# A hybrid decoder block with product-key experts: the scatter of routing weights without accumulation, and 32 instead of 24 tokens by expert rows

## The chip, the cores and the metric

One core of a Trainium2 chip runs the whole program once. The metric is the device time of that core in microseconds (us). A profiled execution gives the trace from which the rows in this text come.

## What is computed

One decoder layer over 512 tokens of width 1024, all in float32: an RMS norm, a joint projection, gated linear attention, sliding-window attention, a gated merge, and then the expert layer, which takes most of the time:

```python
qp = (xt @ w_pq).reshape(t, 8, 2, 128)
scores = einsum('thpd,hpkd->thpk', qp, sub_keys)      # 8 heads, 2 sides, 128 keys
s_top, i_top = top_k(scores, 16)                      # per side
cand = s_top[:, :, 0, :, None] + s_top[:, :, 1, None, :]
best, pos = top_k(cand, 16)                           # 16 experts for each of 8 heads
idx, gate = chosen_experts(pos), softmax(best)        # 128 (expert, weight) pairs per token
h = gelu(einsum('lkd,ld->lk', expert_u[idx], x))
out = einsum('lk,lkd->ld', gate * h, expert_v[idx])   # 16384 experts
```

Two heads of one token can choose the same expert; its weights then add.

## The kernel before

**The experts, two ways.** The 512 tokens are four tiles of 128. Tokens of tile one, and the first `XG` tokens of tile two, go *by expert rows*: for each of a token's 128 experts an indirect DMA fetches that expert's row of U and V side by side (8 KB per token, 1 MB for 128 partitions), VectorE multiplies the U half by the token and sums (`product`, L1339), ScalarE makes the gate, and VectorE adds the gated V half to an accumulator (`addition`, L1356). Tile one takes 128 such *slots* ("v"). The `XG` tokens of tile two are copied `XR = 128 // XG` times over the partitions, so that their 128 experts take only `XS` slots ("y"). With `XG = 24` these are 5 copies, 26 slots, 120 partitions, and 154 slots in all.

The other `TD = 512 - 128 - XG` tokens go *densely*: for each of 128 blocks of 128 experts, `h_step` computes gelu(U·x) of all those tokens (24 matmuls `hp`, line L236, in `proj`), and `v_step` adds V·(weights·h) to eight accumulators (24 matmuls `oa` or `oacc`, L1461). Each number is split in a high and a low part and three products are summed, hence 3 x 8 matmuls of 128x128 weights with `TD` columns. `PHASES` orders the blocks: 88 U blocks, their 88 V blocks, then 20 and 20, then 20 and 20. Each weight block is a 512 KB DMA into `raw`; ScalarE makes its high part `whi`, VectorE its low part `wlo` (L177), some blocks ahead.

**The table of weights.** The dense way needs, for each expert block, a table of 128 experts by tokens that holds the gates. It is built while the first 88 U blocks run. For tokens of tiles two and three VectorE makes two one-hots per token (`onehot`, L1182 and L1185) and TensorE multiplies them (`gmm`, matmuls `gp`, L1198), four tokens at a time, `NGR` groups; ScalarE copies the result to `gbuild` and SyncE writes it to the DRAM tensor `gd`. For tile four the table `g3` lies in DRAM, zeroed early, and GpSimd *scatters* into it: `scatter(h, k)` sends 128 weights, one per token, to the places that `place` computed, with an accumulating indirect DMA (L1153). Within a head a token's experts differ, so its 16 scatters need no order; the first scatter of a head waits for all of the head before (`after`). `HD` says how many scatters are issued after each U block: 16 in 9 blocks. Later `g_load` reads both tables back for four blocks at once (tile `gt`, L1426 and L1427), `w_a` multiplies them with h (L1440, one instruction for each of `PIECES`), and `w_b` makes the low part (L1451).

**The order of the work.** It is written out at build time. `pump` runs steps of the slots between blocks while four counters (`pe`, `dve`, `dma`, `pool`, in estimated us) say that the engines can take them, so an estimate changes the order and nothing else. GpSimd's queue holds scatters and row gathers in one line. In the first stretch at most three row gathers are outstanding (tile `row`, tag `er`); at block 82 all that are outstanding are finished (`while early[0]: step()`), the buffers are freed, and the remaining 126 gathers (tile `rows`, pairs of 2 MB) run beside the V blocks and later U blocks. At block `N0 - GL` = 82 GpSimd issues the first two `g_load`s, which wait for the last head's scatters.

Of the kernel before, what the change touches and what calls it, by code (L numbers as in the profile page):

```python
# [9 lines left out]
F32 = mybir.dt.float32  # L10
# [5 lines left out]
OP = mybir.AluOpType  # L16
# [41 lines left out]
POOLQ = 9.0  # L58
GL = 6

HD = (3, 2, 2, 3, 2, 2, 2, 0, 0)
XG = 24
XR = 128 // XG
XS = -(-128 // XR)
XP_ = XG * XR
# [1 line left out]
TB = 128 - XG  # L67
TD = T - TG

CT, CL = 32, 8  # L70
NGR = (TD - 128) // 4
NCT = (TD - 128 - CL) // CT
GA, GB = NCT * 4 * CT, (1 + 128 // CL) * 4 * CL
# [15 lines left out]
def tile_block(ctx, tc, xT, wst, smalls, wgk2, keysT, uT, vv, uv_rows, out):  # L89
    nc = tc.nc  # L90
# [3 lines left out]
    PS = ctx.enter_context(tc.tile_pool(name="psum", bufs=1, space=PSUM))  # L94
# [102 lines left out]
    for kb in (0, 1, 2, 4, 6):  # L197
        n = 1 if kb < 2 else 2
        nc.sync.dma_start(xt[:, kb:kb + n], xT[:, kb:kb + n])
        if kb < 2:  # L200
            x = slice(kb * 512, kb * 512 + 512)
# [675 lines left out]
    XP = ctx.enter_context(tc.tile_pool(name="xtok", bufs=1, side="left"))  # L877
# [30 lines left out]
    for d in range(9):  # L908
# [12 lines left out]
        if d:  # L921
            p = x1_tail(d - 1)
# [171 lines left out]
    def decode(t):  # L1094
        ij = R.tile([128, 2, 128], F32, name="ij", tag="ij", bufs=2)
        for sd in range(2):
            eq = eq_mult(t, sd)
            yield
            yield from tree(ij[:, sd], eq)
        gf = gate[:, t].rearrange("p h k -> p k h")  # L1100
        if t == 0:
            nc.vector.scalar_tensor_tensor(eidx, ij[:, 0], 128.0, ij[:, 1], OP.mult, OP.add)
            nc.vector.tensor_copy(wgt.rearrange("p (k h) -> p k h", h=8), gf)
            return
        if t == 3:
            nc.vector.tensor_copy(w3.rearrange("p (k h) -> p k h", h=8), gf)
            place(ij)
            return
        eg = R.tile([128, 2, 128], F32, name="eg", tag="eg")
        gk = eg[:, 1]  # L1110
        nc.vector.tensor_copy(gk.rearrange("p (k h) -> p k h", h=8), gf)
        if t == 1:
            nc.vector.scalar_tensor_tensor(eg[:, 0].bitcast(I32), ij[:, 0], 128.0, ij[:, 1], OP.mult, OP.add)

            def copy(r):
                n = min(XS, 128 - r * XS)
                nc.sync.dma_start(misc[r * XG:(r + 1) * XG, 384:384 + 2 * XS].rearrange("p (s k) -> p s k", s=2)[:, :, 0:n],
                                  eg[0:XG, :, r * XS:r * XS + n])

            gout.extend([lambda r=r: copy(r) for r in range(XR)])  # L1120
        yield
        p = PS.tile([128, 3, 128], F32, name="ijp", tag="PT")
        for i, s_ in enumerate((ij[:, 0], ij[:, 1], gk)):
            nc.tensor.transpose(p[:, i], s_, ident)
        ijg = R.tile([128, 3, 128], F32, name="ijg", tag="ijg", bufs=2)
        nc.scalar.copy(ijg, p)
        ijgs[t] = ijg

    addr = XP.tile([128, 128], I32, name="addr")
    scs, heads = [], [[] for _ in range(8)]  # L1130


    def place(ij):
        r4 = R.tile([128, 128], I32, name="r4")
        tk = R.tile([128, 4], I32, name="tk")
        nc.gpsimd.iota(tk[:, 0:1], pattern=[[0, 1]], base=0, channel_multiplier=1)
        nc.vector.tensor_scalar(tk[:, 1:2], tk[:, 0:1], 128 - CL, None, OP.bitwise_and)
        tf = R.tile([128, 4], F32, name="tf")
        nc.vector.tensor_copy(tf[:, 0:2], tk[:, 0:2])
        nc.vector.scalar_tensor_tensor(tf[:, 2:3], tf[:, 1:2], 3.0, tf[:, 0:1], OP.mult, OP.add)  # L1140
        nc.vector.tensor_copy(r4, ij[:, 0])
        nc.vector.tensor_scalar(r4, r4, 3, None, OP.bitwise_and)
        a = ij[:, 1]
        nc.vector.scalar_tensor_tensor(a, ij[:, 0], 32.0, a, OP.mult, OP.add)
        nc.vector.tensor_scalar(a, a, 512.0, tf[:, 2:3], OP.mult, OP.add)
        f = R.tile([128, 128], F32, name="pf")
        nc.vector.tensor_copy(f, r4)
        nc.vector.scalar_tensor_tensor(addr, f, CL - 16384.0, a, OP.mult, OP.add)

    def scatter(h, k):  # L1150
        c = k * 8 + h
        nc.gpsimd.nop()
        i = nc.gpsimd.indirect_dma_start(  # L1153
            out=g3, out_offset=bass.IndirectOffsetOnAxis(ap=addr[:, c:c + 1], axis=0), in_=w3[:, c:c + 1],
            in_offset=None, compute_op=OP.add).ins
        tc.declare_no_dep(i, group=f"head{h}", reason="a token's experts differ within a head")
        tc.add_to_no_dep_group(f"head{h}", i)
        heads[h].append(i)
        if h and k == 0:
            after(i, h - 1)  # L1160
        pool[0] += 2.3
        xfer(0.33)

    def after(i, h):
        for o in heads[h]:
# [7 lines left out]
    def xfer(us):  # L1173
        dma[0] += us / DUTY
# [14 lines left out]
    def gmm(n):  # L1189
# [3 lines left out]
        if q == 0:  # L1193
            gbs[c] = Dn.tile([128, 128, CT if c < NCT else CL], F32, name="gbuild", tag="gbuf", bufs=2)
        o = hot.pop(n)
        p = PS.tile([128, 4, 128], F32, name="gp", tag=("M2", "M3", "O")[n % 3])
        for k in range(4):
            nc.tensor.matmul(p[:, k], o[:, 0, k], o[:, 1, k], start=True, stop=True)  # L1198
        nc.scalar.copy(gbs[c].rearrange("p i t -> p t i")[:, q * 4:q * 4 + 4, :], p)
# [10 lines left out]
    def route():  # L1210
# [31 lines left out]
        next(d3, None)  # L1242
        dve[0] += 4.5
        scs.extend((h, k) for h in range(8) for k in range(16))
        yield
        d1 = decode(1)
        for c in (2.4, 0.9, 0.5, 2.7, 0.9, 0.5):
# [297 lines left out]
    for ph, (b0, b1) in enumerate(PHASES):  # L1545
        vo = VORD[ph]
        for b in range(b0, b1):
# [29 lines left out]
            if scs:  # L1577
                b_s = min(b_s, b)
                k = HD[(b - b_s) % len(HD)]
                for x in scs[:k]:  # L1580
                    scatter(*x)
                del scs[:k]
# [121 lines left out]
```

## Time and profile before

| | us |
|---|---|
| median of 3 runs (lowest, highest) | 1742.1 (1736.7, 1749.2) |
| profiled execution, its own time | 1741.63 |
| span from first to last instruction in it | 1739.9 |
| TensorE busy | 1706.3 (98%) |
| VectorE busy | 1323.4 (76%) |
| ScalarE busy | 768.1 (44%) |
| GpSimd busy | 708.8 (41%) |

The dense part begins 636 us into the span. By the stretches of the trace, 655 to about 1031 us is the table stage (U blocks with one-hots, scatters and 28 row gathers); then V blocks until about 1401, U to 1480, V to 1560, U to 1640, V to the end. TensorE's busy time comes from modelled ends of pipelined matmuls, so the distance between starts tells what a matmul costs. Profile rows read: line, engine, operation, tile written <- tiles read, shape, count | busy us, mean ns of one | idle us before them and what ended it. In the chain of waits and in timelines a row begins with its start and its length in us.

### The profile page before, as it was taken

The numbers are of one execution on the slowest core, as the hardware profiler recorded it, in microseconds if no ns is written. First come the engines' busy times: TensorE is split into PE (matmuls) and PEld (weight loads), VectorE is DVE, ScalarE is ACT, GpSimd is POOL, SyncE is SP. The second block draws the span as 40 slices with busy tenths as digits, with TensorE's granted clock in tenths as the row PEclk, the third lists the DMA queues.
The fourth block names the chain that finished last, engine by engine and source line by source line (L and its number), as shares of the span: only waits on it lengthen the run. The fifth ranks groups of instructions, "written<-read, shape, count | busy, mean of one in ns | idle before, by whom it ended". The sixth has DMA issues, their size and how long they took to land.

```text
span 1739.9 us, 26384 instructions
## 1 busy us (share of the span) xinstructions
PE 1706.3 (98%) x9858; PEld 1580.5 (91%) x9858; DVE 1323.4 (76%) x2568; ACT 768.1 (44%) x1356; POOL 708.8 (41%) x451
## 2 busy tenths in 40 slices
PE   9999999999999999999999989999999999989998
PEld 7776688988887899999999989999999999989998
DVE  7767624347248999888778748999989988898895
ACT  5545523335345234455555434444444454444441
POOL 0003444534544453778788772222212232233320
PEclk9999999999999999999999999999999999999999
DMA  5324532222343335799999899999999999998983
GB/s 173 97 61 121 150 117 85 71 76 72 97 154 122 112 119 151 189 296 303 282 297 295 244 287 388 413 411 414 411 409 382 384 388 396 360 383 352 376 356 119
DMA packets 164548, 431.20 MB, mean 248 GB/s; under 512 B 34757, under 2 KB 80709, under 8 KB 144325
## 3 DMA queue, kind: packets, MB, share of 16 engines
q1 hardware_dynamic: 118597, 253.95, 42.1%
q0 software_dynamic: 40928, 163.04, 26.6%
q10 hardware_dynamic: 4896, 12.54, 1.9%
q8 instruction: 77, 1.26, 0.3%
q14 instruction: 50, 0.41, 0.1%
HBM read 388.57 MB, written 40.88 MB: 247 GB/s over the span
## 4 chain that ended last, share of the span: by engine, by line
PE 72%; DVE 13%; DMA 6%; issue 3%; ACT 3%; POOL 2%; SPq 0%; DVEq 0%; ACTq 0%; POOLq 0%
PE oa L1461 19%; PE hp L236 18%; PE mm L236 16%; PE mm L253 6%; PE oacc L1461 6%; DMA rows<-in_uv_rows_dram,misc 3%; PE gp L1198 2%; DVE wlo L177 2%; POOL g L1153 2%; DMA raw<-in_vv_dram 1%; DVE w L976 1%; DMA row<-in_uv_rows_dram,misc 1%; DVE accv L1356 1%; DVE idx L974 1%; DVE idx L980 1%
## 5 line engine op out<-in xcount | busy, mean ns | idle before, releaser
L167 ACT CAST whi<-raw 128x1024 fp32r<-128x1024 f32 x347 | 361.4, 1045 | 141.0 <-DMA raw<-in_vv_dram 51.0
L1324 POOL DMA_INDIRECT rows<-in_uv_rows_dram,misc x126 | 173.0, 1373 | 464.5 <-DVE accv L1356 370.2
L177 DVE TENSOR_TENSOR wlo<-raw,whi 128x1024 fp32r<-128x1024 f32 x268 | 326.1, 1219 | 46.5 <-issue 21.3
L236 PE MATMUL hp<-xh,whi 128*128 128x360 f32 x1024 | 342.4, 334 | 7.0 <-ACT ev L1515 4.4
L236 PE MATMUL hp<-xh,wlo 128*128 128x360 f32 x1024 | 337.4, 329 | 8.7 <-DVE wlo L177 8.7
L236 PE MATMUL hp<-xl,whi 128*128 128x360 f32 x1024 | 336.3, 328 | 0.0
L1153 POOL DMA_INDIRECT g<-w,addr x128 | 252.8, 1975 | 86.5 <-issue 39.6
L177 POOL TENSOR_TENSOR wlo<-raw,whi 128x1024 fp32r<-128x1024 f32 x79 | 194.1, 2461 | 157.0 <-ACT whi L167 152.0
L1461 PE MATMUL oa<-wh,whi 128*128 128x360 f32 x768 | 251.2, 327 | 2.3 <-ACT ring L1408 2.3
L1461 PE MATMUL oa<-wh,wlo 128*128 128x360 f32 x768 | 251.9, 328 | 0.9 <-DVE wlo L177 0.8
L1461 PE MATMUL oa<-wl,whi 128*128 128x360 f32 x768 | 251.4, 327 | 0.0
L236 PEld LDWEIGHTS hp<-xh,wlo 128*128 128x128 f32 x1024 | 193.8, 189 | 10.5 <-DVE wlo L177 10.5
L236 PEld LDWEIGHTS hp<-xh,whi 128*128 128x128 f32 x1024 | 194.0, 189 | 8.4 <-ACT ev L1515 4.7
L236 PEld LDWEIGHTS hp<-xl,whi 128*128 128x128 f32 x1024 | 194.0, 189 | 0.0
L1461 PEld LDWEIGHTS oa<-wh,whi 128*128 128x128 f32 x768 | 144.9, 189 | 2.6 <-ACT ring L1408 2.6
L1461 PEld LDWEIGHTS oa<-wh,wlo 128*128 128x128 f32 x768 | 144.5, 188 | 1.8 <-DVE wlo L177 1.8
L1461 PEld LDWEIGHTS oa<-wl,whi 128*128 128x128 f32 x768 | 144.9, 189 | 0.0
L1295 ACT ACTIVATE misc<-misc 128x1 f32<-128x1 f32 (+1 forms) x154 | 31.3, 203 | 245.5 <-DVE rows L1339 186.6
L1356 DVE SCALAR_TENSOR_TENSOR accv<-rows,misc,accv 128x1024 f32<-128x1024 f32 x100 | 127.9, 1279 | 15.4 <-ACT misc L1296 15.4
L1339 DVE SCALAR_TENSOR_TENSOR rows<-rows,xtok 128x1024 f32<-128x1024 f32 x100 | 121.9, 1219 | 8.1 <-DMA rows<-in_uv_rows_dram,misc 7.9
L236 PE MATMUL mm<-hhi,whi 128*128 128x512 f32 x256 | 103.9, 406 | 0.0
L236 PE MATMUL mm<-hhi,wlo 128*128 128x512 f32 x256 | 99.9, 390 | 0.0
(599 smaller groups left out, 3296.5 us busy)
## 6 DMA issues: line engine op xcount, KB each, us to landing
raw<-in_uT_dram SPq DMA_DIRECT2D x128, 512.0 KB, 6.2
raw<-in_vv_dram SPq DMA_DIRECT2D x128, 512.0 KB, 8.8
raw<-in_wst_dram SPq DMA_DIRECT2D x92, 512.0 KB, 3.5
gd<-gbuild SPq DMA_DIRECT2D x56, 256.0 KB, 7.6
gt<-gd SPq DMA_DIRECT2D x30, 464.0 KB, 7.5
hs<-hw ACTq DMA_DIRECT2D x34, 360.0 KB, 3.0
ring<-hs SPq DMA_DIRECT2D x34, 360.0 KB
g<-zero SPq DMA_DIRECT2D x16, 512.0 KB, 5.8
```

The source lines that it names most:

```text
L167: nc.scalar.copy(hi, self.raw[u])
L177: self.lo_eng(u).tensor_tensor(lo, r, hi.bitcast(F32), OP.subtract)
L236: nc.tensor.matmul(ps[:, :n], a[:, kb, :], b[:, kb, c0:c0 + n], start=(kb == 0 and i == 0), stop=(kb == KB - 1 and i == 2))
L253: nc.tensor.matmul(banks[t], a[:, kb, t * 128:(t + 1) * 128], b[:, k, :], start=(first and k == 0 and i == 0), stop=(last and k == kk - 1 ...
L974: nc.vector.max_index(ix[:, 0:8], v[:, 0:8], src)
L1153: i = nc.gpsimd.indirect_dma_start(out=g3, out_offset=bass.IndirectOffsetOnAxis(ap=addr[:, c:c + 1], axis=0), in_=w3[:, c:c + 1], in_offse ...
L1198: nc.tensor.matmul(p[:, k], o[:, 0, k], o[:, 1, k], start=True, stop=True)
L1295: nc.scalar.activation(h, h, AF.Gelu)
L1324: nc.gpsimd.indirect_dma_start(out=rows[n], out_offset=None, in_=uv_rows, in_offset=bass.IndirectOffsetOnAxis(ap=ix[:, slots[n][1]:slots[n ...
L1339: nc.vector.scalar_tensor_tensor(cur, cur, 1.0, xs_[kind][0:m, :], OP.mult, OP.mult, accum_out=hc)
L1356: nc.vector.scalar_tensor_tensor(a_, cur, h_[0:m, s_:s_ + 1], a_, OP.mult, OP.add)
L1461: nc.tensor.matmul(accs[c][:, 0:TD], v_[:, cs], a, start=(first and i == 0), stop=(last and i == 2))
```

## The change

Two things are changed. First, tile four's scatters no longer accumulate: they write. So that the last writer of a place has the full weight, VectorE computes for head h and choice k the sum of the weights of all choices of heads 0 to h that name the same expert (`same`, one `scalar_tensor_tensor` over `16h + 16` columns that compares the token's addresses `key` with this one, multiplies by the weights `con`, which lie in a PSUM bank, and sums). Head 0 needs none, so there are 112. They are issued 6 scatters ahead. The columns of `addr` and `w3` go by head now, `HD` is 16 scatters in 8 blocks, and the planner's estimates for a scatter are lower. `con` keeps PSUM bank "O", so the `gp` results alternate over two banks instead of three. The one-hots themselves are as before.

Second, `XG` is 32: 4 copies, 32 "y" slots on all 128 partitions, 160 slots in all; `TD` is 352, `NGR` 56 instead of 58. With `CL = 32` the table is one piece: seven chunks of 32 tokens (before: seven of 32 and one of 8), `w_a` is one multiplication over 704 columns instead of two over 448 and 272.

```diff
-HD = (3, 2, 2, 3, 2, 2, 2, 0, 0)
-XG = 24
+HD = (3, 2, 3, 2, 3, 2, 1, 0)
+XG = 32
...
-CT, CL = 32, 8
+CT, CL = 32, 32
...
         if t == 3:
-            nc.vector.tensor_copy(w3.rearrange("p (k h) -> p k h", h=8), gf)
+            con.append(PS.tile([128, 2, 128], F32, name="con", tag="O"))
+            nc.scalar.copy(con[0][:, 0], iof)
+            nc.vector.tensor_copy(con[0][:, 1].rearrange("p (h k) -> p h k", h=8), gate[:, t])
+            nc.vector.tensor_copy(w3[:, 0:16], gate[:, t, 0])
             place(ij)
...
-        nc.vector.scalar_tensor_tensor(addr, f, CL - 16384.0, a, OP.mult, OP.add)
+        hk = lambda v: v.rearrange("p (k h) -> p h k", h=8)
+        nc.vector.scalar_tensor_tensor(key.rearrange("p (h k) -> p h k", h=8), hk(f), CL - 16384.0, hk(a), OP.mult, OP.add)
+        nc.vector.tensor_copy(addr, key)
+
+    def same(h, k):
+        n, c = 16 * h + 16, 16 * h + k
+        if h:
+            nc.vector.scalar_tensor_tensor(dump[:, 0:n], key[:, 0:n], key[:, c:c + 1], con[0][:, 1, 0:n],
+                                           OP.is_equal, OP.mult, accum_out=w3[:, c:c + 1])
+            dve[0] += 0.14 + n / 960
 
     def scatter(h, k):
-        c = k * 8 + h
+        c = h * 16 + k
         nc.gpsimd.nop()
         i = nc.gpsimd.indirect_dma_start(
             out=g3, out_offset=bass.IndirectOffsetOnAxis(ap=addr[:, c:c + 1], axis=0), in_=w3[:, c:c + 1],
-            in_offset=None, compute_op=OP.add).ins
+            in_offset=None).ins
...
-        pool[0] += 2.3
-        xfer(0.33)
+        pool[0] += 1.4
+        xfer(0.2)
...
-        p = PS.tile([128, 4, 128], F32, name="gp", tag=("M2", "M3", "O")[n % 3])
+        p = PS.tile([128, 4, 128], F32, name="gp", tag=("M2", "M3")[n % 2])
...
                 k = HD[(b - b_s) % len(HD)]
+                n = max(0, k + 6 - len(scs) + len(sums))
+                for x in sums[:n]:
+                    same(*x)
+                del sums[:n]
                 for x in scs[:k]:
                     scatter(*x)
```

**GpSimd, end of the table stage.** `g_79` is the table `g3`, `row` an early gather, `gt` the first `g_load`, `rows` the later gathers. Before, scatters and gathers alternate up to the first `g_load`:

```order
L1153 DMA g_79<-w_3941,addr 2097152x1 x5
L1324 DMA row<-in_uv_rows_dram,misc 128x2048
L1153 DMA g_79<-w_3941,addr 2097152x1 x2
L1324 DMA row<-in_uv_rows_dram,misc 128x2048
L1153 DMA g_79<-w_3941,addr 2097152x1 x4
L1426 DMA gt<-gd 128x928
```

With the change:

```order
L1167 DMA g_79<-w_3941,addr 2097152x1 x5
L1339 DMA row<-in_uv_rows_dram,misc 128x2048
L1167 DMA g_79<-w_3941,addr 2097152x1 x3
L1339 DMA row<-in_uv_rows_dram,misc 128x2048
L1167 DMA g_79<-w_3941,addr 2097152x1 x3
L1339 DMA row<-in_uv_rows_dram,misc 128x2048 x6
L1441 DMA gt<-gd 128x896
L1442 DMA gt<-g_79 128x512
L1441 DMA gt<-gd 128x896
L1442 DMA gt<-g_79 128x512
L1339 DMA rows<-in_uv_rows_dram,misc 128x2048 x126
```

The last scatter stands ahead of the last six early gathers now, and not directly ahead of `gt`. The early gathers are 34 instead of 28; the later ones are 126 in both.

**VectorE, table stage, three blocks.** `wlo` is a block's low part, `oh` are the one-hots, `eq` is the decoding of the next tile. Before:

```order
L177 TENSOR_TENSOR wlo_6332<-raw_6247,whi_6282 128x1024
L1087 TENSOR_TENSOR eq<-pb,clo 128x2048
L1091 TENSOR_TENSOR eq<-eq,idd 128x2048
L1182 TENSOR_TENSOR oh<-iof,ijg 128x512
L1185 TENSOR_SCALAR oh<-iof,ijg 128x128 x4
L177 TENSOR_TENSOR wlo_6396<-raw_6284,whi_6334 128x1024
```

With the change:

```order
L177 TENSOR_TENSOR wlo_6359<-raw_6267,whi_6307 128x1024
L1087 TENSOR_TENSOR eq<-pb,clo 128x2048
L1091 TENSOR_TENSOR eq<-eq,idd 128x2048
L1196 TENSOR_TENSOR oh<-iof,ijg 128x512
L1199 TENSOR_SCALAR oh<-iof,ijg 128x128 x4
L1160 SCALAR_TENSOR_TENSOR dump,w_3941<-key,con 128x48 x3
L177 TENSOR_TENSOR wlo_6418<-raw_6309,whi_6361 128x1024
```

Two or three sums stand between a block's one-hots and the next low part, in nearly every block of the stage.

**VectorE, the end.** `accy` is the last accumulator, `wr` and `wl` are the products for the V blocks. Before, the last addition stands seven low parts ahead of the end:

```order
L1356 SCALAR_TENSOR_TENSOR accy<-rows,misc,accy 120x1024 x2
L1440 TENSOR_TENSOR wr<-ring,gt 128x2x224
L1440 TENSOR_TENSOR wr<-ring,gt 128x2x136
L177 TENSOR_TENSOR wlo_15959<-raw_15890,whi_15924 128x1024
L1451 TENSOR_TENSOR wl<-wr,wh 128x720
L177 TENSOR_TENSOR wlo_15991<-raw_15926,whi_15961 128x1024
```

With the change it stands ahead of the last one:

```order
L1371 SCALAR_TENSOR_TENSOR accy<-rows,misc,accy 128x1024
L1466 TENSOR_TENSOR wl<-wr,wh 128x704
L177 TENSOR_TENSOR wlo_16183<-raw_16112,whi_16152 128x1024
L1371 SCALAR_TENSOR_TENSOR accy<-rows,misc,accy 128x1024
L177 TENSOR_TENSOR wlo_16212<-raw_16154,whi_16185 128x1024
L1540 TENSOR_TENSOR yT<-yT,oa 128x352 x3
```

The same 126 later slots are spread over 166 instead of 159 blocks.

More of the change, by code (lines that the diff above doesn't have):

```diff
@@ L1129, in tile_block @@
     addr = XP.tile([128, 128], I32, name="addr")
-    scs, heads = [], [[] for _ in range(8)]
+    scs, con, sums, heads = [], [], [], [[] for _ in range(8)]
+    key = XP.tile([128, 128], F32, name="key")
+    dump = XP.tile([128, 128], F32, name="dump")
     def place(ij):
@@ L1244, in route @@
         scs.extend((h, k) for h in range(8) for k in range(16))
+        sums.extend(scs)
         yield
```

## The prediction

> **What bounds the kernel now.** I read the page first, then the busy times by stage, then what TensorE waits for.
>
> ```profile
> span 1739.9 us, 26384 instructions
> PE 1706.3 (98%) x9858; PEld 1580.5 (91%) x9858; DVE 1323.4 (76%) x2568; ACT 768.1 (44%) x1356; POOL 708.8 (41%) x451
> ...
> PE 72%; DVE 13%; DMA 6%; issue 3%; ACT 3%; POOL 2%; SPq 0%; DVEq 0%; ACTq 0%; POOLq 0%
> ```
>
> TensorE (PE) makes 72% of the chain that ended last, and no other engine has a fifth of that. A PE that is busy by modelled ends may still issue slowly, so I count starts. The stages, each with busy us and instruction counts, and at the row's end the granted clock, DMA share and GB/s:
>
> ```profile
> core 0: us, PE busy (x) PEld busy (x) DVE busy (x) ACT busy (x) POOL busy (x), PEclk, DMA share, GB/s
> 700.00:970.00 270.00, 269.26 (x1760) 268.64 (x1759) 211.41 (x404) 142.79 (x205) 216.72 (x120) 1.00 0.96 277
> 970.00:1040.00 70.00, 62.11 (x372) 60.78 (x371) 42.62 (x62) 29.65 (x51) 53.27 (x35) 0.95 0.95 258
> 1040.00:1480.00 440.00, 440.00 (x2683) 440.00 (x2682) 399.66 (x493) 196.31 (x351) 108.19 (x82) 1.00 1.00 399
> 1480.00:1660.00 180.00, 172.47 (x1025) 170.91 (x1024) 160.02 (x197) 77.61 (x152) 54.93 (x39) 0.97 0.96 370
> ```
>
> From 1040 to 1480 us 2683 matmuls start in 440 us, one every 164.0 ns without a hole: there PE is the bound, beside a VectorE (DVE) at 91% and a DMA share of 1.00. Two stages have holes. In 1480 to 1660, 1025 matmuls at 164 ns need 168 us, so 12 are lost. In 970 to 1040 some of the 372 are narrow:
>
> ```profile
> L1198 PE MATMUL gp<-oh 128*128 128x128 f32 x52 | 6.9, 274 | 0.0
> ...
> 1010.00:1020.00 10.00, 6.20 (x25) 5.90 (x24) 5.18 (x6) 2.16 (x5) 8.47 (x6) 0.68 0.74 181
> ```
>
> 320 at 164 ns and 52 table products at 101 ns (their own price is below) are 57.7 us, so 12.3 of 70 are lost, most of them in the ten us of the second row, where PE stands idle and then runs at a lower clock (0.68 in the mean). Why, GpSimd's (POOL's) rows say:
>
> ```profile
> 678.15 2.46 POOL L1153 DMA_INDIRECT g<-w,addr  x1 [26.73 <-DVE addr L1148]
> ...
> 1019.69 1.98 POOL L1324 DMA_INDIRECT row<-in_uv_rows_dram,misc  x1 [0.30 <-issue]
> ...
> 1028.59 2.14 POOL L1153 DMA_INDIRECT g<-w,addr  x1 [0.30 <-issue]
> ```
>
> ```profile
> DVE row L1339 <- DMA row<-in_uv_rows_dram,misc: 65.0, 18, 11.1
> ```
>
> From 678 to 1031 us POOL does nothing but issue scatters and row gathers in one line, 0.30 us apart. The last early gather leaves at 1020, though the program wants all of them finished before block 82. DVE waits 65.0 us in this stage for rows that stand behind scatters; its queue is in order, so at the end PE's next low part waits behind it.
>
> **The dense matmuls, 360 to 352 columns.** The price per column comes from the two widths, in the chain of waits (start, length, count):
>
> ```profile
> 290.95 10.89 PE mm L236 x48
> ...
> 410.61 80.24 PE mm L236 x348
> ...
> 1401.76 78.78 PE hp L236 x480
> ```
>
> With 360 columns a matmul takes 78.78/480 = 164.1 ns, with 512 between 226.9 (x48) and 230.6 (x348). The slope is 0.41 to 0.44 ns per column, so 8 columns are 3.3 to 3.5 ns. There are 6144 dense matmuls (256 blocks of 24): 20.3 to 21.5 us, all where PE sets the pace. I take **-20.3**; 14.3 of it is in the 181 blocks from 1031 us on.
>
> **Two table groups fewer.** Eight passes of one group hold PE from 944.00 to 944.81, 101 ns each:
>
> ```profile
> 944.00 1.05 PE L1198 MATMUL gp<-oh 128*128 128x128 f32 x8
> 944.81 0.41 PE L236 MATMUL hp<-xh,whi 128*128 128x360 f32 x1
> ```
>
> Two groups are **-1.6**. Two `gp` banks instead of three make a product wait for the evacuation two groups back, about 10 us earlier, with ScalarE at 143 of 270 us: nothing, unless ScalarE runs 10 us late. SyncE issues eight table writes fewer, nothing on the path.
>
> **The scatters on POOL.** The trace has no plain scatter. Nearest are the accumulating one and the row gather, which also has 128 addresses:
>
> ```profile
> L1153 POOL DMA_INDIRECT g<-w,addr x128 | 252.8, 1975 | 86.5 <-issue 39.6 <-DVE addr L1148 26.7 <-DMA g<-w,addr 19.9
> L1324 POOL DMA_INDIRECT row<-in_uv_rows_dram,misc x28 | 31.4, 1123 | 8.5 <-issue 7.0 <-DVE oh L1185 1.2 <-DVE wlo L177 0.3
> ...
> 904.22 1.00 POOL L1324 DMA_INDIRECT row<-in_uv_rows_dram,misc  x1 [0.30 <-issue]
> 905.52 4.11 POOL L1153 DMA_INDIRECT g<-w,addr  x1 [0.31 <-DMA g<-w,addr]
> 909.94 1.55 POOL L1153 DMA_INDIRECT g<-w,addr  x1 [0.30 <-issue]
> ```
>
> Ends: 1.00 us (a gather) and 1.98 (no saving). An undisturbed accumulating scatter takes 1.55, the mean is 0.43 above it. I take the gather's 1.00 and the same 0.43, **1.43**, as both instructions build 128 addresses. The line is then 678 + 128 x (1.43 + 0.30) + 34 x 1.42 + 20 of waits between heads = 967 us; at 1.98 it is 1038. Block 82 comes at about 1031 - 12.3 - 7 = 1012. So POOL is ahead by 45 us, the early rows have landed, and most of the 12.3 goes: **-9.5**, as one wait at the flush may stay.
>
> The long scatter is explained by what DVE does beside it:
>
> ```profile
> 908.11 1.12 DVE L1185 TENSOR_SCALAR oh<-iof,ijg 128x128 f32<-128x128 f32 x4
> ```
>
> [...] The trace agrees: the 4.11 us scatter spans these one-hots, the 1.55 us one follows them. [...]
>
> **The 112 sums on DVE.** Nearest rows:
>
> ```profile
> 677.56 0.29 DVE L1148 SCALAR_TENSOR_TENSOR addr<-pf,ij 128x128 int32<-128x128 f32 x1
> ...
> L1339 DVE SCALAR_TENSOR_TENSOR row<-row,xtok 128x1024 f32<-128x1024 f32 x28 | 34.2, 1222 | 65.0 <-DMA row<-in_uv_rows_dram,misc 65.0
> ...
> L1339 DVE DVE_READ_ACCUMULATOR row<-row,xtok 128x1 f32 x28 | 2.3, 80 | 0.0
> ```
>
> 0.29 at 128 and 1.22 at 1024 columns give 1.04 ns per column and 0.16 fixed; the sums have 80 columns on average: 0.24, with 0.08 to read the accumulator **0.32**. Each writes `dump` behind its predecessor, so a wait may come on top: ends 0.20 (reads overlapped) and 0.44. In 700 to 970 DVE is idle 58.6 of 270 us; the stretch shrinks by 6, leaving 52.6. New there: 103 sums x 0.32 = 33, six more slots at 1.22 + 0.08 + 1.27 = 15.4, less 3.5 for two one-hot groups: 45. It fits, with 8 us over, but not evenly, and the waits for rows don't all vanish. I charge **+5** (0 to 25). Before 700 DVE has no such cover:
>
> ```profile
> 655.00:700.00 45.00, 42.28 (x254) 41.36 (x252) 43.76 (x75) 18.05 (x24) 19.11 (x10) 1.00 0.52 150
> ```
>
> DVE is busy 43.8 of 45 us and PE already waits. About eight sums and two copies more in `place` are **+2.8**. A late sum also holds back its scatter, and with it POOL's line; the lead of six scatters is about three blocks, 14 us.
>
> A row of a VectorE instruction with a PSUM input, as `con` is:
>
> ```profile
> L1534 DVE TENSOR_TENSOR xr<-xr,yt 104x128 f32<-104x128 f32 x8 | 2.2, 281 | 0.8 <-PE yt L1533 0.7
> ```
>
> [...]
>
> **The late part.** 126 slots as before, with less time per block.
>
> ```profile
> L1440 DVE TENSOR_TENSOR wr<-ring,gt 128x448 f32<-128x448 f32 x64 | 39.5, 617 | 0.0
> L1440 DVE TENSOR_TENSOR wr<-ring,gt 128x272 f32<-128x272 f32 x64 | 27.7, 432 | 0.0
> ```
>
> One product over 704 columns is 617 + 256 x 1.05 = 886 ns instead of 1049: DVE gets 10 us back over 64 pairs, while PE gives it 14.3 less, so its share stays near 91%. The slots are spread over 166 blocks instead of 159, at 3.85 instead of 3.93 us: one in 5.1 us, before one in 5.0; so the DMA rate of 399 GB/s hardly changes either. I leave the 12 us of holes after 1480 as they are: 0. The last addition now stands before the last low part instead of seven before the end: **+1**.
>
> **Sum.** -20.3 - 1.6 - 9.5 + 5 + 2.8 + 1 = -22.6. The profiled execution took 1741.6 us (span 1739.9 and 1.7 around it), 0.5 below the median of the runs: **1719**.
>
> **Rivals.** *DVE becomes the bound in the table stage.* At 0.44 the 103 sums cost 45, the new work 57 against a cover of 52.6, and if half of the waits for rows stays, PE is some 22 us late instead of 5: 1736. It decides from 0.40 us per sum. For it: the 43.8 of 45. Against: 58.6 us idle now.
>
> *Slower: POOL stays the bound.* If a plain scatter costs 1.98, the line ends at 1038 with six gathers still to issue; three buffers let them go in two rounds of about 9 us, and block 82 is left at 1056, 25 after now. The blocks behind save 14.3: 1741.6 + 25 - 14.3 = 1752. It crosses zero at about 1.9 us. For it: nothing here shows that accumulation is what costs. Against: the gather's 1.00.
>
> *The late part gives nothing back.* At a DMA share of 1.00 the V blocks may be paced by transfers; then 14.3 are lost: 1733. For it: 399 GB/s. Against: 2683 starts without a hole.
>
> *More is gained.* If DVE's cover suffices and the holes after 1480 shrink by 8: 1706.
>
> *The change doesn't do what it says*, if matmul time didn't follow the width; the rows for 360 and 512 exclude it.
>
> **How the numbers follow.** Forecast 0.57 (its own range 1708 to 1730); DVE bound 0.18; late part 0.09; more gained 0.09; POOL bound 0.07. A measurement here tells about 1%, 17 us, from no change. Faster by over 1%, below 1724.7: three quarters of the forecast, the greater gain and a little of the DVE case, 0.54. Slower by over 1% needs the POOL case beyond its price: 0.04. The rest, 0.42, is within 1%. The range runs from 1702 to 1741: its low end is the greater gain, its high end the DVE case with a few us more; only the POOL case lies outside.
>
> **What would show it.** Right: about 160.8 ns between dense matmuls; scatters of 1.2 to 1.6 us; the last early gather before block 82 and no hole there; sums of 0.3 us and DVE nearly full from 700 to 970. Wrong: PE waiting for low parts all through 700 to 970 (DVE), scatters near 2 us (POOL), or PE holes between 1040 and 1480 (transfers).

## The result and the profile after

The changed kernel takes 1702.1 us (median of 4 runs, 1696.5 to 1704.4), the kernel before 1741.9 beside it: a ratio of 0.9759 (95% interval 0.9722 to 0.9796), some 40 us where I forecast 22.6. The direction was right; the gain was nearly twice as large, and the time lies on the low end of my range. The profiled execution took 1700.7 us. Its page:

```profile
span 1698.9 us, 26519 instructions
PE 1671.8 (98%) x9842; PEld 1544.4 (91%) x9842; DVE 1351.8 (80%) x2738; ACT 767.5 (45%) x1367; POOL 655.0 (39%) x456
...
PE 67%; DVE 18%; DMA 8%; issue 4%; ACT 3%; POOL 1%; DVEq 0%; ACTq 0%; POOLq 0%
```

The stages, in the same columns as before:

```profile
core 0: us, PE busy (x) PEld busy (x) DVE busy (x) ACT busy (x) POOL busy (x), PEclk, DMA share, GB/s
655.00:700.00 45.00, 41.21 (x247) 40.23 (x245) 43.66 (x79) 19.46 (x27) 18.44 (x14) 0.96 0.46 146
700.00:970.00 270.00, 265.70 (x1759) 263.63 (x1760) 252.58 (x635) 144.70 (x216) 185.33 (x139) 0.99 0.89 297
970.00:1040.00 70.00, 69.41 (x451) 69.12 (x451) 49.85 (x65) 33.93 (x60) 22.61 (x18) 1.00 0.99 359
1040.00:1480.00 440.00, 438.87 (x2755) 438.01 (x2754) 403.25 (x456) 200.31 (x355) 121.13 (x82) 1.00 1.00 398
1480.00:1660.00 180.00, 176.84 (x1100) 175.02 (x1099) 167.05 (x197) 81.20 (x159) 58.31 (x40) 1.00 1.00 399
```

Three things differ from the rows of before. From 1040 to 1480 there are 2755 starts instead of 2683, one every 159.7 ns instead of 164.0. From 970 to 1040 PE is busy for 69.4 of 70 us instead of 62.1: the hole before block 82 is gone. And from 700 to 970 DVE is busy 252.6 us instead of 211.4, with PE still at 265.7. The groups that I had priced (line, engine, operation, count, busy us, mean ns, idle before):

```profile
L1167 POOL DMA_INDIRECT g<-w,addr x128 | 168.8, 1318 | 94.0 <-issue 41.2 <-DVE addr L1155 27.2 <-DMA g<-w,addr 14.6
L1160 DVE SCALAR_TENSOR_TENSOR dump<-key,con 128x32 f32<-128x32 f32 (+6 forms) x112 | 33.0, 295 | 2.3
L1160 DVE DVE_READ_ACCUMULATOR dump<-key,con 128x1 f32 x112 | 9.3, 83 | 0.0
L1455 DVE TENSOR_TENSOR wr<-ring,gt 128x704 f32<-128x704 f32 x64 | 56.8, 887 | 0.0
```

A scatter takes 1.32 us (1.43 predicted, 1.98 before), a sum 295 + 83 = 378 ns (320 predicted), the joined product 887 ns (886 predicted). The wait for rows, 65.0 us before, is nearly gone:

```profile
DVE row L1354 <- DMA row<-in_uv_rows_dram,misc: 6.4, 4, 2.6
```

To split the 41.0 us between the two spans I take all distances between starts of PE. *Pauses* are what a distance exceeds the usual one for its width by, where that is over 40 ns; the rest is the pace. With the pauses left out the 6144 dense matmuls stand 164.6 ns apart before and 159.2 after: 5.4 x 6144 = 33.1 us. The two table groups are 1.6. Pauses by stretch (about 4 us from 710 to 970 are the regular steps between narrow and wide matmuls):

| us of pauses | 650-710 | 710-970 | 970-1040 | 1040-1480 | 1480 to the last low parts |
|---|---|---|---|---|---|
| before | 4.4 | 4.6 | 11.9 | 0 | 12.2 |
| after | 7.8 | 11.6 | 1.4 | 1.9 | 4.8 |

That is 5.6 less; 33.1 + 1.6 + 5.6 = 40.3 of the 41.0. With the last few us of each program, a run's pauses are 36.3 us before and 30.5 after; these totals are compared below.

### The profile page after: what moved, and what is told of

Read it like the earlier page. It is cut to its first block, busy times and chain, and to the rows that moved or that the text cites. A ratio compares the mean times of both kernels' runs of the same rounds, so it can differ in the third digit from the quotient of the medians.

```text
span 1698.9 us, 26519 instructions
## 1 busy us (share of the span) xinstructions
PE 1671.8 (98%) x9842; PEld 1544.4 (91%) x9842; DVE 1351.8 (80%) x2738; ACT 767.5 (45%) x1367; POOL 655.0 (39%) x456
## 4 chain that ended last, share of the span: by engine, by line
PE 67%; DVE 18%; DMA 8%; issue 4%; ACT 3%; POOL 1%; DVEq 0%; ACTq 0%; POOLq 0%
PE hp L236 17%; PE mm L236 17%; PE oa L1476 15%; PE mm L253 7%; PE oacc L1476 5%; DVE wlo L177 3%; DMA raw<-in_vv_dram 3%; DMA rows<-in_uv_rows_dram,misc 2%; PE gp L1212 2%; DMA row<-in_uv_rows_dram,misc 2%; DVE accv L1371 1%; DVE w L976 1%; DMA raw<-in_uT_dram 1%; DVE rows L1354 1%; DVE wr L1455 1%
## 5 line engine op out<-in xcount | busy, mean ns | idle before, releaser
L1339 POOL DMA_INDIRECT rows<-in_uv_rows_dram,misc x126 | 183.6, 1457 | 455.4 <-DVE accv L1371 329.4
L236 PE MATMUL hp<-xh,whi 128*128 128x352 f32 x1024 | 336.1, 328 | 2.2 <-ACT ring L1423 0.8
L236 PE MATMUL hp<-xh,wlo 128*128 128x352 f32 x1024 | 331.8, 324 | 5.5 <-DVE wlo L177 4.5
L236 PE MATMUL hp<-xl,whi 128*128 128x352 f32 x1024 | 330.4, 323 | 0.5 <-issue 0.5
L1476 PE MATMUL oa<-wh,wlo 128*128 128x352 f32 x768 | 247.4, 322 | 1.8 <-DVE wlo L177 1.8
L1476 PE MATMUL oa<-wh,whi 128*128 128x352 f32 x768 | 247.6, 322 | 1.6 <-ACT ring L1423 1.6
L1476 PE MATMUL oa<-wl,whi 128*128 128x352 f32 x768 | 247.0, 322 | 0.6 <-DVE wl L1466 0.6
L1167 POOL DMA_INDIRECT g<-w,addr x128 | 168.8, 1318 | 94.0 <-issue 41.2
L1371 DVE SCALAR_TENSOR_TENSOR accv<-rows,misc,accv 128x1024 f32<-128x1024 f32 x94 | 120.5, 1282 | 17.3 <-ACT misc L1311 17.1
L1310 ACT ACTIVATE misc<-misc 128x1 f32<-128x1 f32 x160 | 32.8, 205 | 206.0 <-DVE rows L1354 183.8
```

What stands on the lines that cost most here:

```text
L236: nc.tensor.matmul(ps[:, :n], a[:, kb, :], b[:, kb, c0:c0 + n], start=(kb == 0 and i == 0), stop=(kb == KB - 1 and i == 2))
L1167: i = nc.gpsimd.indirect_dma_start(out=g3, out_offset=bass.IndirectOffsetOnAxis(ap=addr[:, c:c + 1], axis=0), in_=w3[:, c:c + 1], in_offse ...
L1310: nc.scalar.activation(h, h, AF.Gelu)
L1339: nc.gpsimd.indirect_dma_start(out=rows[n], out_offset=None, in_=uv_rows, in_offset=bass.IndirectOffsetOnAxis(ap=ix[:, slots[n][1]:slots[n ...
L1371: nc.vector.scalar_tensor_tensor(a_, cur, h_[0:m, s_:s_ + 1], a_, OP.mult, OP.add)
L1476: nc.tensor.matmul(accs[c][:, 0:TD], v_[:, cs], a, start=(first and i == 0), stop=(last and i == 2))
```

## The experiments

### The two parts alone

`plain24` is the change with `XG = 24` and `CL = 8`; `acc32` is the kernel before with `XG = 32` and `CL = 32`.

> The scatter part of the change alone: plain scatters, sums, their pace and their banks, with 24 tokens by rows as before (360 columns, 58 groups, two pieces). Theory 'the parts add' (the matmuls got cheaper by the width alone): the hole at the flush goes, -11.5 us, against the new holes at 655 to 710 and at 748, +10.8; a dense matmul stays at 164.6 ns: 1738 to 1744 us; if the holes after 1480 shrink too, 1735. Theory 'the accumulating scatters slowed the matmuls': the matmuls of the table stage go from 165.7 to 164 or below, and the time is 1730 or less. My prediction's own terms give -9.5 + 5 + 2.8: 1740.

> The token part of the change alone: 32 tokens by rows (352 columns, 56 groups, one piece), with the accumulating scatters, their pace and three banks as before. Theory 'the parts add' with the measured matmul: 6144 x 5.4 ns = -33.1, groups -1.6, six more gathers in GpSimd's line at 1.42 us = +8.5 at the flush: 1715 us, and a dense matmul takes 159.2 ns; if the hole after 1560 goes as well, 1710. With the 3.3 ns of my prediction it would be 1728.

`plain24` took 1729.7 us, 0.9897 of before (0.9849 to 0.9946), `acc32` 1733.8, 0.9918 (0.9886 to 0.9950). By these ratios the parts together give about 10 us more than their sum, which is no more than the intervals leave open. Of the three theories on record for `plain24` only the second allows so large a gain, and that one is out as well, since a matmul of its table stage takes 165.7 ns as before: its pauses fell from 36.3 to 24.4 us, those before 970 hardly grew although the sums are there, and DVE's wait for rows is 0.2 us. `acc32` missed the other way: its matmuls take 160.2 ns (27 us less), but in the profiled execution (1738.6 us, above the median) its pauses grew from 36.3 to 62.3 us. VectorE waits 55.5 us for rows, and the end looks like this:

```profile
1690.00:1737.00 47.00, 29.29 (x136) 23.06 (x134) 40.28 (x64) 7.66 (x23) 11.65 (x7) 0.77 0.67 249
```

```profile
rows<-in_uv_rows_dram,misc POOLq DMA_INDIRECT x135, 9.0
```

PE works 29 of the last 47 us and DVE 40: with the dearer scatters in its account the planner let 25 rows go early and left 135 for the late part, and DVE finishes them after PE has run out of blocks. With the cheap scatters in the account it is 34 and 126. So the lower estimate for a scatter is of use at 32 tokens, if it is what moves the 9 rows; that was not tried alone. I had taken the 126 as given.

### What the sums do

`nosum` is the changed kernel with all gates copied to `w3` and `if h:` replaced by `if False:`, so neither sum nor count. `charge` leaves out the sums and keeps the planner's count of their time, `nocharge` keeps the sums and leaves out the count, and `freesum` sums into a tile that nobody reads; in `charge` and `freesum` all gates are copied to `w3` too. The part of `charge` at the sums:

```diff
         if h:
-            nc.vector.scalar_tensor_tensor(dump[:, 0:n], key[:, 0:n], key[:, c:c + 1], con[0][:, 1, 0:n],
-                                           OP.is_equal, OP.mult, accum_out=w3[:, c:c + 1])
             dve[0] += 0.14 + n / 960
```

> The changed kernel without the 112 sums (equal experts of two heads are not added: the last weight written stands); the scatters are plain and the order of all else is made by the same rules. Theory 'VectorE' (the hole at 748 and the waits before 710 come from VectorE, which the sums fill): both go, 7.4 + 3.4 us, 1690 us. Theory 'transfers' (at 741 three row gathers of 1 MB leave at once and a weight block stands behind them): the hole at 748 stays, only the 3.4 us go, 1697 us. If the sums cost nothing: 1701.

> The changed kernel without the 112 sums, as before, but the planner still counts their time (0.14 us + n/960 each) in its estimate of VectorE. Without the sums and without that count the kernel took 1736 us, VectorE waited 56.4 us for rows in the table stage, and TensorE waited behind it. Theory 'the account' (the count makes the planner place a row's product later, when the row has landed): the waits for rows fall below 15 us, and the time to 1690 to 1700. Rival 'the sums themselves fill the time' (what a waiting VectorE loses, it loses in either order): the waits stay near 50 us and the time stays above 1725.

> The changed kernel, its sums and their count kept, but each sum goes to a scratch tile that nobody reads and the scatters send the plain gates (equal experts of two heads are not added), so that no scatter waits for a sum. Against 1702 us with everything, 1716 with the count alone, 1736 with neither. Theory 'occupied' (VectorE, filled by the sums, comes to a product later, when its row has landed): VectorE's waits for rows stay below 15 us and the time is 1699 to 1706. Rival 'held back' (the sums help because the scatters wait for them): the waits return to about 43 us and the time to 1713 to 1720.

> The changed kernel, everything computed, but the planner does not count the sums' time (36 rows go early instead of 34, 124 late). Theory 'occupied alone is enough': the sums fill VectorE whatever the planner thinks, its waits for rows stay below 15 us, and the time is 1698 to 1706. Rival 'both are needed' (without the count the products are placed too early, and the low parts behind them are late): waits above 30 us, 1712 to 1725.

| | sums | count | median us | ratio to before (95%) | DVE waits for rows, us | pauses, us |
|---|---|---|---|---|---|---|
| `nosum` | no | no | 1736.0 | 0.9965 (0.9932 to 0.9998) | 56.4 | 59.3 |
| `charge` | no | yes | 1716.0 | 0.9849 (0.9809 to 0.9890) | 43.1 | 44.9 |
| `nocharge` | yes | no | 1709.8 | 0.9824 (0.9767 to 0.9882) | 15.2 | 34.9 |
| `freesum` | yes, unread | yes | 1702.3 | 0.9762 (0.9700 to 0.9823) | 6.4 | 30.7 |
| the change | yes | yes | 1702.1 | 0.9759 (0.9722 to 0.9796) | 6.4 | 30.5 |

Waits and pauses are those of the profiled execution, which for `charge` took 1723.6 us. All of my theories for `nosum` were wrong: taking 42 us of work from DVE made the kernel 34 us slower, nearly as slow as before, although a scatter takes 1.59 us there instead of 1.98. `charge` came out halfway between its two theories, `nocharge` a little below its rival. In `nosum` DVE waits for rows, and PE for what stands behind DVE (total us, times, longest):

```profile
DVE row L1354 <- DMA row<-in_uv_rows_dram,misc: 56.4, 13, 8.5
PE hp L236 <- DVE wlo L177: 11.8, 8, 3.1
PE hp L236 <- ACT hw L1423: 5.9, 4, 3.3
```

One place in the timeline of `nosum` shows how (start, length, engine, operation, and in brackets the idle time before it):

```profile
921.93 2.47 POOL L1339 DMA_INDIRECT row<-in_uv_rows_dram,misc  x1 [0.30 <-DVE oh L1199]
...
932.02 1.23 DVE L1354 SCALAR_TENSOR_TENSOR row<-row,xtok 128x1024 f32<-128x1024 f32 x1 [7.44 <-DMA row<-in_uv_rows_dram,misc]
...
933.17 1.22 DVE L177 TENSOR_TENSOR wlo<-raw,whi 128x1024 fp32r<-128x1024 f32 x1
933.29 0.20 ACT L1310 ACTIVATE misc<-misc 128x1 f32<-128x1 f32 x1 [5.96 <-DVE row L1354]
933.53 0.29 ACT L1311 ACTIVATE misc<-misc 128x1 f32<-128x1 f32 x1
933.73 0.45 ACT L1423 ACTIVATE hw<-hp 128x352 f32<-128x352 f32 x1
```

A row that left POOL at 922 lands at 932. DVE has reached its product at 924.6 and stands for 7.4 us. Behind the product, in DVE's queue, stands the next block's low part; behind the gate, in ScalarE's queue, stands the gelu that frees PE's bank. PE pauses for 3.5 us at 930.6, and the granted clock is 0.68 in the mean from 930 to 938. With the sums DVE arrives later, when the row is there: after the first six rows a product starts 9 to 17 us after its gather in nearly all rows of the changed kernel and of `freesum`, and mostly 7 to 12 us after it in `nosum` and `charge`, where many of these times hold a wait for the landing. From issue to landing a row took 8.5 us in the median of the early rows before and 7.5 in `acc32`; the one above took 10.1. `freesum`, in which no scatter waits for a sum, behaves as the change does, so it is the filled DVE that helps and not that scatters are held back; `nocharge` shows that the filling alone gives 26 of the 34 us and the planner's count, which places products later, the other 8. Without the sums the count gives 20.

### The distance without the change

`before_charge` and `before_land` are the kernel before with one edit each; `nosum_land` has the second edit on `nosum`:

```diff
+                for h, _ in scs[:k]:
+                    dve[0] += (0.14 + (16 * h + 16) / 960) * (h > 0)
...
-LAND = 14.0
+LAND = 20.0
```

> The kernel before with one edit: at each scatter the planner adds to its estimate of VectorE what a sum would cost (0.14 us + n/960), though there are no sums. Everything is computed as before. Theory 'the account' (much of what the change gained outside the matmuls comes from products that are placed later, not from the cheaper scatters): the waits of VectorE for rows fall from 65.0 us to below 20, the hole at 1010 shrinks, and the time falls by 8 to 12 us, to 1730 to 1734. Rival 'the scatters' (GpSimd's line is what is late): rows are late whatever the order, the hole at 1010 stays, and the time is 1738 to 1750.

> The kernel before with one number changed: the planner takes 20 instead of 14 us for a row to land before it places the product (24 instead of 28 rows go early, 130 instead of 126 late). Theory 'distance' (VectorE's order reaches a product before its row has landed, and the next low part stands behind it; what the sums and their count brought was distance): the 65.0 us of waits for rows fall below 25, the hole at 1010 to 1030 mostly goes, and the time falls by 6 to 10 us, to 1734 to 1738. Rival 'GpSimd's line' (the accumulating scatters make the rows late by more than 20 us before the flush): the waits stay above 45 us and the time is 1741 or more.

> The changed kernel without the sums and without their count (1736 us with 56.4 us of waits for rows), with 20 instead of 14 us for a row to land (30 instead of 36 rows early). Theory 'distance': the waits fall below 15 us, the 28 us of holes from 820 to 1010 go, and the time is 1695 to 1710, the level that the changed kernel has with the sums. Rival 'the sums': it needs the sums as such (they hold the scatters back, or keep VectorE level): the time stays above 1720.

`before_charge`: 1745.8 us, 1.0008 (0.9975 to 1.0040), with 69.5 us of waits: the rival. The result is the rival's, but it doesn't decide for the rival's reason: the count moved hardly anything here (28 rows early in both, the last gather at 1020 in both). `before_land`: 1730.8 us, 0.9918 (0.9885 to 0.9951):

```profile
DVE row L1339 <- DMA row<-in_uv_rows_dram,misc: 13.3, 5, 6.4
```

```profile
970.00:1040.00 70.00, 67.04 (x413) 66.74 (x412) 35.91 (x46) 29.95 (x49) 46.70 (x31) 0.98 0.92 282
```

The scatters still take 1.89 us and the last one leaves at 1020, and yet 11.9 us of pauses around the flush became 5.2, and the kernel gained as much as `plain24`. So more than half of the hole goes with scatters as dear as before. That products stood too close behind their gathers is the likelier reason, since the waits for rows fell from 65.0 to 13.3 us; but four gathers fewer also make GpSimd's line about 6 us shorter (4 x 1.42; the last scatter left at 1029 before), and no run parts the two. `nosum_land` failed its theory: 1726.4 us, 0.9886 (0.9817 to 0.9955), and 50.4 us of waits. Its distances are still 8 to 13 us in most rows after the first stretch, since the planner adds its 20 us to an estimated issue that counts 1.4 us for a scatter while scatter and step take 1.56 + 0.30. That this is why it failed is read from the trace and was not tried.

### The width of a matmul

`ladder`, `u_after`, `u_before` and `u_start` change the width and first column in the U blocks, by block number or by phase, for instance:

```diff
-        ps = proj(w, XN, n=TD, c0=TG, bank=bank, each=each)
+        n, c0 = (360, 152) if b < 88 else (344, 168) if b < 108 else (368, 144)
+        ps = proj(w, XN, n=n, c0=c0, bank=bank, each=each)
```

> The changed kernel, but the matmuls of the 128 U blocks take ten widths and start columns in turn (block number modulo 10): 352 from column 160 (as in the change), 352 from 156, 352 from 152, 356 from 156, 360 from 152 (as before the change), 360 from 144, 364 from 148, 368 from 144, 376 from 136, 384 from 128. Gelu always reads the first 352 columns of the bank, so in nine of ten blocks h belongs to shifted tokens; the amount of all other work is the same. To be told apart is why a dense matmul went from 164.6 to 159.2 ns where the slope of 0.43 ns per column gives 3.4 less. Theory 'step' (the width is charged in steps of 16 columns): 352 takes 159 ns wherever it starts, 356, 360, 364 and 368 all take 165 to 166, 376 and 384 about 172. Theory 'start' (a first column that is no multiple of 16 costs more): 352 from 160 takes 159, from 156 and 152 about 162; 360 from 144 takes 162.5 and from 152 about 165. Theory 'slope' (the width is charged by the column, and what slowed the kernel before was other work beside the matmuls): 352 takes 159 anywhere, 356 161, 360 162.5 from either column, 364 164.3, 368 166, 376 169.5, 384 173.

> The changed kernel with other widths in the U blocks, the same through a whole phase: 360 columns from 152 in blocks 0 to 87, 344 from 168 in 88 to 107 (h is then right for the wrong tokens, and 8 columns are taken twice), 368 from 144 in 108 to 127; V blocks keep 352. Theory 'the width' (a steady stream of 352 is cheaper than the slope says, whatever kernel it stands in): in the first phase 360 columns take 165.5 ns or more between starts as before the change, 368 takes 167 to 168. Rival 'the kernel' (the changed kernel lets all matmuls run faster): 360 takes 162 to 163. For 344 the slope from 352 gives 155.2 ns, a step below it 151 to 152.

> The kernel before with other widths in the U blocks: 352 columns from 160 in blocks 0 to 87, 352 from 152 in 88 to 107, 360 from 144 in 108 to 127 (where the columns don't match the tokens, h belongs to others, and 8 columns are taken twice in the first two); V blocks keep 360. Theory 'the width': 352 takes 158.5 to 159.5 ns from either column although all else is as before, 360 from 144 takes 163.6 or more. Rival 'the kernel': 352 takes 161 or more. Rival 'the start': 352 from 160 takes 159, from 152 162 or more, and 360 from 144 less than the 163.6 that it takes from 152.

> The changed kernel with other start columns and widths in the U blocks: 352 from 152 in blocks 0 to 87, 344 from 160 in 88 to 107, 352 from 144 in 108 to 127 (h belongs to other tokens; in the second 8 columns are taken twice). V blocks keep 352 from a start that is a multiple of 16. Theory 'start': 352 from 152 takes 162 to 163 ns in all stretches, from 144 158.5 to 159.5, 344 from 160 155 to 156. Theory 'state' (the same matmuls run at one of two paces, and a stall may change it): 352 from 152 takes 158.5 to 160 in the mean of the 88 blocks, the values of single stretches differ by 3 to 7 ns whatever the start, and V of the same shape shows 159.2 in one phase and 161.5 in another.

Their times (1712.8, 1713.4, 1736.8 and 1707.3 us, one run each) are of little use; the paces count. In one and the same stretch of the table stage, first the kernel before, then the change, then `u_after` with 360 columns, all with 8 narrow matmuls for every 24 to 26 wide ones:

```profile
800.00:900.00 100.00, 100.00 (x658) 100.00 (x657) 76.11 (x142) 54.09 (x81) 79.45 (x45) 1.00 1.00 296
```

```profile
800.00:900.00 100.00, 100.00 (x679) 99.98 (x678) 99.16 (x248) 58.13 (x89) 76.16 (x55) 1.00 0.99 334
```

```profile
800.00:900.00 100.00, 100.00 (x657) 100.00 (x657) 96.55 (x240) 55.22 (x85) 72.28 (x52) 1.00 0.96 328
```

With 360 columns the changed kernel starts as few matmuls as the kernel before, and with 352 from 160 `u_before` is as fast as the change: it is the matmul's own columns, their number and the first one, and not what else the change does. Mean distance between starts of U matmuls, pauses left out:

| columns, from | ns, and where |
|---|---|
| 344 from 160 / from 168 | 157.6 (`u_start`, late) / 159.4 (`u_after`, late) |
| 352 from 160 | 159.0 (after, table stage), 159.3 (`u_before`, table stage), 158.5 (after, late) |
| 352 from 144 / from 152 | 160.3 (`u_start`, late) / 161.4 (`u_start`, table stage), 162.9 (`u_before`, late) |
| 360 from 152 | 165.7 (before, table stage), 165.3 (`u_after`, table stage), 163.9 (before, late) |
| 360 from 144 / 368 from 144 | 165.8 (`u_before`, late) / 167.2 (`u_after`, late) |
| `ladder`, change at every block | 352: 160.3 to 162.6; 360: 164.3 to 166.6; 368: 167.8; 376: 173.0; 384: 174.8 |

In a steady stream 352 columns from 160 take 5.4 to 6.7 ns less than 360 from 152 in the same stage, while from 368 to 360 it is 1.4 to 3.3. The change moves the first column too, and 352 from 152 takes 161.4 in the table stage: so 2.4 ns of the difference there may belong to the start. No theory on record fits it all. The means show no steps of 16 columns, since 360 (163.9 to 166.6 ns) lies below 368 (167.2 and 167.8). A first column that is no multiple of 16 goes with 1 to 4 ns more at 344 and 352. Late in the kernel it is the other way at 360 (163.9 from 152, 165.8 from 144), and in `ladder` it is so at 360 (166.4 and 164.5) and not at 352 (162.5 from 160, 161.9 from 152, 160.4 from 156). In `ladder`, where the width changes with each block, the means lie within 2 ns of a line again, 161.6 at 352 and 174.8 at 384 or 0.41 ns per column. The trace of before has a third width besides 360 and 512, matmuls of 256 columns in its chain of waits (start, length, count):

```profile
238.30 11.51 PE mm L253 x96
```

They take 11.51/96 = 119.9 ns. From there to the late 360 (164.1) the slope is 0.43, as it is from 360 to 512.

Part of the scatter is that one shape runs at two paces. `nosum`, V matmuls of 352 columns, before and after two pauses, of 1.7 us at 1153 and 0.8 us at 1166:

```profile
1050.00:1150.00 100.00, 100.00 (x628) 99.75 (x628) 89.26 (x102) 43.23 (x73) 23.69 (x16) 1.00 1.01 404
1200.00:1300.00 100.00, 100.00 (x620) 100.00 (x620) 90.24 (x103) 45.04 (x74) 23.21 (x16) 1.00 1.02 406
```

> The changed kernel itself, a second profile. In the first profile the V matmuls of 352 columns took 159.3 ns in the first two V phases and 161.6 in the last, in other kernels 161.5 in the first. Theory 'state' (which of two paces a stretch runs at is not fixed by the program): at least one V phase changes its pace, by 2 ns or more. Rival 'program' (addresses and order fix it): 159.3, 159.3, 161.6 again.

The first and the second profile of the changed kernel, last V phase:

```profile
1625.00:1685.00 60.00, 60.00 (x375) 59.93 (x374) 56.43 (x68) 23.73 (x43) 9.12 (x6) 1.00 0.79 306
```

```profile
1625.00:1685.00 60.00, 60.00 (x382) 59.77 (x381) 56.33 (x73) 23.65 (x42) 9.26 (x6) 1.00 0.75 289
```

The second (1697.0 us) shows 159.5 ns where the first had 161.6, by the same program; the other V phases are 159.2 to 159.3 in both. So the program doesn't fix the pace. That a pause changes it is not shown: in `nosum` the change follows the two pauses, and in the first profile pauses at 1610 and 1617, but the second has pauses of 1.0 us at 1608 and 1615 and keeps its pace.

Block by block (24 matmuls) the two paces are plainer than as means. In the last V phase four blocks in turn take 166.3, 160.9, 158.9 and 160.1 ns per matmul in the first profile, and 158.3, 160.0, 158.4 and 160.2 in the second: the slower pace is for the most part one block in four that takes 8 ns more. In `ladder` the 13 blocks of 352 from 160 lie at 158.2 to 160.2 (six) or at 163.4 to 166.7 (seven). In the kernel before, with 360 columns, more than half of the blocks of the table stage take 166.2 ns or more, and most late U blocks 163.3. So a mean over a stage tells how often each value occurs, and a line through means need not hold for the next width. What decides between the values is open.

Over all dense matmuls of a run 352 columns took 159.1 to 160.5 ns in nine profiles, 360 took 164.5 to 164.6 in four. The narrower matmul, with the first column that comes with it, is worth 25 to 34 us.

### The new pause at 748

The first profile of the change has a pause that before has not:

```profile
741.56 0.96 POOL L1339 DMA_INDIRECT row<-in_uv_rows_dram,misc  x1 [0.30 <-issue]
...
742.82 0.94 POOL L1339 DMA_INDIRECT row<-in_uv_rows_dram,misc  x1 [0.31 <-issue]
...
743.71 1.23 DVE L177 TENSOR_TENSOR wlo<-raw,whi 128x1024 fp32r<-128x1024 f32 x1 [3.06 <-issue]
...
755.28 1.23 DVE L177 TENSOR_TENSOR wlo<-raw,whi 128x1024 fp32r<-128x1024 f32 x1 [8.22 <-issue]
```

Three rows of 1 MB leave within 3 us, and from 741 to 748 the DMA queue that brings weight blocks moves nothing (5 packets, 0.00 MB); VectorE stands idle for 8.2 us before the next low part. `stagger` lets one row go first, then two:

```diff
-            while not held[0] and n < min(n_, k + 3 + 2 * end[0]):
+            while not held[0] and n < min(n_, k + min(3, k + 1) + 2 * end[0]):
```

> The changed kernel with the first three row gathers not issued at once but one, then two more after the first row is done (31 rows early, 129 late). Theory 'transfers' (the hole at 740 to 755 comes from 3 MB of rows that leave within 3 us ahead of a weight block): the hole goes, no other comes, and the time falls by 5 to 8 us, to 1694 to 1697. Rival 'VectorE' (it is late by the sums whatever the rows do): the hole stays or moves, and the time is 1700 to 1705.

It took 1705.6 us, 0.9778 (0.9718 to 0.9838). The pause is gone, but three more rows are left for the late part and as many us of pauses stand there (at 1099 and 1677); no gain. And `after_again` hasn't the pause either, without the edit, so its absence in `stagger` shows nothing of its cause. No experiment beat the change.

## Why the prediction was right and wrong, step by step

- **The width: -20.3 predicted, -33.1 measured.** This is the step that failed: "The slope is 0.41 to 0.44 ns per column, so 8 columns are 3.3 to 3.5 ns." Measured are 5.4 ns. Of the 2.1 ns that are missing 0.5 lie at the kernel before (164.6 ns over all dense matmuls, where I took the late 164.1) and 1.6 at the change (159.2 instead of the 160.8 that I named). The line itself wasn't badly drawn. The 256 columns of the same trace lie on it, and between them and 360 it gives 160.7 at 352. What failed is to read one width's pace off a line: in the table stage 360 columns stand above it (165.7 ns against 163.9 late), and 352 in their better pace stand below it. Where either comes from isn't settled. That PE sets the pace in the late part was right (the rival "gives nothing back" is out): the mechanism stands, the size of this term was 12.8 us short. A slip beside it, without weight: 174 blocks are left at 1031 us (6 U blocks of the first phase, its 88 V blocks and the last 80), not 181, so the late share is 13.8 us and not 14.3.
- **The hole at the flush: -9.5 predicted, -10.5 measured, and only in part for the reason given.** I wrote "So POOL is ahead by 45 us, the early rows have landed, and most of the 12.3 goes". POOL is ahead, but by some 15 us: its last scatter leaves at 976 (before at 1029), the last early gather, which waits for a free buffer, at 1000, and block 82 begins at 1016. And being ahead is not enough: in `nosum` the last scatter leaves at 995, and 7.2 us of the hole are still there, with 32 us of pauses from 710 to 1040, while `before_land` keeps the dear scatters and loses over half of the hole. With cheap scatters in both, `charge` has 8.2 us of pauses from 970 to 1040 and `freesum` 0.5: there the distance from gather to product decides. That the number came so near is luck.
- **The sums: +5 and +2.8 predicted.** The price (378 ns, not 320) came near the 0.40 from which I had DVE as the bound, and still that rival failed. Before 710 the pauses are 4.4 us before, 6.1 in `plain24` with the sums alone, 6.3 in `acc32` with the narrower matmuls alone, and 7.8 with both: so the sums cost about 1.6 us there, and a TensorE that needs its next low part earlier costs the rest. After that I looked for room in which to hide them, and didn't see that idle DVE time was itself the trouble: it was DVE standing at rows. In the first profile 7.0 us of pauses came there, in the second none; taking the sums away costs 14 us, with their count 34.
- **The late part: 0 predicted, -5.5 measured** (-3 in the second profile). A 4.4 us pause of before at 1561, where the eviction of an accumulator stood behind a gate that waited for a row, isn't there. A pause of this kind is in `plain24`, `nosum` and `before_land` too (5.0, 8.6 and 5.4 us) and hardly in `stagger` (1.4): it depends on where a row falls, and I can't claim it for the change.
- **Groups, product and end** (-1.6, 886 ns, +1): as predicted, but for the end, which costs nothing.

So of the 18 us missed 12.8 are the matmuls' width and most of the rest the late part. "More is gained" at 1706 was the nearest case, with a chance of 0.09; that the time lies near it is luck, since the gain has other sources than that case had.

## What to carry to other kernels

Measure the pace of a matmul at the width that you go to, as one kernel with that width alone; a line through other widths gave 20 of the 33 us here. Where an engine's work stands in one queue, as a low part stood behind a product that waited 7.4 us for its row in `nosum`, look at the distance between a transfer's issue and the instruction that uses it before you look at how long the issuing engine is busy: one number in the planner of the kernel before (20 instead of 14 us) is worth 0.8%. And read idle time of an engine by what ends it: work put into it can be free or better, if the engine otherwise stands at a transfer with the critical engine's input queued behind (42 us of sums on DVE, with their count, took 34 us off here).

## What the runs showed of the hardware that I had not expected

Matmuls of one shape and program ran at two paces, 159.2 or 161.3 ns in V blocks of 352 columns in `nosum`; in the changed kernel's last V phase it was 161.6 in one profile, with one block in four at 166.3, and 159.5 in the other, with that block at 158.3. What switches them is open. At 360 columns V blocks showed 164.1 in each of four profiles. A scatter of 128 single words without accumulation took 1.32 us on GpSimd (1.59 in `nosum`, beside a DVE without sums; why is open), with accumulation 1.89 (`before_land`, `acc32`) to 1.98 (before).
